# One set of 512-column value products per token mixer, and another order of the projections around it

## The chip, the core and the metric

The kernel runs on one core of a Trainium2 chip. It has five engines that each work through an instruction stream of their own in order: TensorE (PE, matrix products; its weight loads are listed as PEld), VectorE (DVE), ScalarE (ACT), GpSimd (POOL) and SyncE (SP, which here issues nearly all transfers). They wait for one another by semaphores. Products are accumulated in PSUM, a memory of eight banks; everything else lies in SBUF. The metric is the time of one execution on the device, in microseconds (us), and lower is better.

## The reference

Two layers; in each, three token mixers read one normalized input, are merged by sigmoid gates, and are followed by a gated feed-forward block and a gated per-layer input. The change touches the projections `h @ w_in` (in its eight parts), the values `va` and `vc` above all, and the gated product of the convolution.

```python
D_MODEL = 1024; SEQ = 512; DEPTH = 2
HA = 4; DH_A = 64; DV_A = 128; WIDTH_A = 512     # differential attention
CB = 512; CONV_W = 31                            # convolution
HC = 8; DC = 64; WIDTH_C = 512                   # neighbourhood attention
...
    for i in range(DEPTH):
        h = rmsnorm(x, norm_mix[i])
        proj = h @ w_in[i]
        qa, ka, va, glu_in, qc, kc, vc, gates = jnp.split(proj, SPLITS, axis=-1)
        ya = diff_attention(qa, ka, va, lam_q1[i], lam_k1[i], lam_q2[i], lam_k2[i],
                            subln_g[i], lam_init, cos, sin)
        yb = conformer_conv(glu_in, conv_w[i], conv_b[i], cln_g[i], cln_b[i])
        yc = neighbourhood_attention(qc, kc, vc, rpb[i])
        ga, gb, gc = jnp.split(jax.nn.sigmoid(gates), 3, axis=-1)
        merged = (ga * (ya @ w_br_a[i]) + gb * (yb @ w_br_b[i])
                  + gc * (yc @ w_br_c[i]))
        x = x + merged @ w_o[i]
        h = rmsnorm(x, norm_ffn[i])
        x = x + (jax.nn.silu(h @ w_ffn_gate[i]) * (h @ w_ffn_up[i])) @ w_ffn_down[i]
        h = rmsnorm(x, norm_ple[i])
        x = x + jax.nn.sigmoid(h @ w_ple_gate[i]) * (p[i] @ w_ple_in[i])
    return rmsnorm(x, norm_final)
```

In `conformer_conv` the input is first gated, `z = a * sigmoid(g)`, and then convolved along the sequence with 31 taps for each channel. `neighbourhood_attention` has eight heads that the kernel treats in four pairs; `diff_attention` has four heads, whose queries and keys are rotated (rope).

## The kernel before, in words

**Precision.** Every operand of a product is held as a high part and a remainder (suffixes h and l, or hi and lo), and a product is three matmuls: high by high, high by remainder, remainder by high. ACT makes the high part of a weight tile (`wh`, from the loaded `wr`), DVE the remainder (`wl`); each of the three tags has three buffers. A projection (`proj`, `gemm`) gives one [128, 512] result: 8 parts of the model width by 3 matmuls of 512 columns, so 24 matmuls. These are the lines L178, L179 and L180.

**PSUM.** The eight banks are shared out by tags: "mm" has three, "sc" (scores) two, "tr" (transposes) two, "av" (outputs of the attention units) one. A tag hands its banks out in turn, so a new accumulator waits until the one that had the bank three times ago has been read.

**Values.** `values` makes the values of half a mixer's heads: 256 columns, two accumulators of the "mm" tag that each hold two row tiles, 8 parts of the width by 4 row tiles by 3 matmuls of 256 columns (L574, L576, L578): 96 matmuls. It is called twice per mixer (`natten_v(0)`, `natten_v(1)`, `diff_v(0)`, `diff_v(1)`). In the names of the trace these are `natten_mm` and `diff_mm`, like the query and key projections.

**Queries and keys.** `natten_in(pr)` projects a pair's queries and keys. ACT makes the high part (`kh`) out of PSUM and DVE the remainder (`natten_t`), and SP then copies both into stacks (`qk`, `x`) from which the scores are made. For pair 0 of a layer, DVE first multiplies the projection by the row scale (`glu_r` or `ple_r`), since the normalization is not yet applied to the input there; this is what frees the projection's bank. `diff_in(head)` copies the projection by ACT into a buffer of the tag "rp" (`diff_rp`, two buffers, one each for a query or a key); SP copies 32-row blocks for the rotation, DVE multiplies and adds, and the remainder takes the same buffer again, from which SP copies it into the stacks.

**Order.** The order of PE is the order of the code. Attention units (`natten_unit`, `diff_unit`: scores, softmax, transposes, output products) are generators that `later` puts in a queue with a delay in ticks; a tick passes after every four chunks (twelve matmuls of 512 columns) of projection work, so units are dealt out between the projections. The orders of the other engines come from a scheduler that takes their instructions by priority; the convolution's taps (`conv_z`, L161 on DVE) are dealt out behind other instructions by `background`.

**The mixers' stage.** First `glu` makes the four gated blocks of the convolution (j = 0 to 3; each projects a gate and a value), then come the neighbourhood pairs and values, then the differential heads and values, then the gates c and b (`gate_c(m)` and `gate_b(m)`, one projection each).

## Time and profile before

| what | value |
|---|---|
| median of 3 runs (lowest, highest) | 1801.88 us (1801.6, 1803.25) |
| the profiled execution | 1801.18 us, of which the span is 1799.4 us |
| instructions in the span | 27361 |
| PE busy | 1780.7 us, 10404 matmuls |
| DVE busy | 1380.7 us, 2140 instructions |
| ACT busy | 893.1 us, 1495 instructions |
| transfers | 255.98 MB, 142 GB/s |

In the rows of the profile, a name such as `natten_mm` is the phase and the tag of a tile with its number left out, and `a<-b` reads "a is written from b". The span is what the profiler covers; the execution's own time is 1.8 us longer. Busy time of PE is a sum of intervals that overlap in part: the next matmul begins before the last one ends. A timeline row has the start, the duration, the engine, the line and the names, and in brackets the idle time of the engine ahead of it with what ended it; a row of the waits has the sum, the number of times and the longest.

### The profile page before, as it was taken

What the parts mean: (1) busy time and instruction counts of PE and PEld (TensorE: products, weight loads), DVE (VectorE), ACT (ScalarE), POOL (GpSimd) and SP (SyncE); (2) the same over time, 40 slices, a digit from 0 to 9 for tenths busy, and PEclk for the clock granted to TensorE, in tenths of its full rate; (3) what the DMA queues carried; (4) which work ended last, traced back from release to release, by engine and by line L of the source; (5) the groups of instructions that cost most, each with busy time, mean ns of one, the idle gap of its engine ahead of it and who ended that gap; (6) DMA issues with size and microseconds to landing.
All of it is one profiled execution on the core that took longest, in us unless ns stands there. A gap on an engine that the chain in (4) does not pass through costs nothing. (4 is left out here: it accounts for less than half of the span.)

```text
span 1799.4 us, 27361 instructions
## 1 busy us (share of the span) xinstructions
PE 1780.7 (99%) x10404; PEld 1573.4 (87%) x10404; DVE 1380.7 (77%) x2140; ACT 893.1 (50%) x1495; POOL 64.1 (4%) x102
## 2 busy tenths in 40 slices
PE   9999999999999999999999999999999999999998
PEld 7888888888889899898888888888888998998987
DVE  7878887897877577577777878878887775765776
ACT  5467455325565245255545755553255552543554
POOL 0000000000001000000000000000000100000000
PEclk9999999999999999999999999999999999999999
DMA  5566561325646466253437656523374662764432
GB/s 199 165 189 164 150 161 42 103 91 177 198 111 187 138 155 186 81 145 115 157 123 188 187 153 161 128 62 100 97 225 129 156 186 82 192 175 112 115 109 94
DMA packets 98099, 255.98 MB, mean 142 GB/s; under 512 B 12976, under 2 KB 18480, under 8 KB 97968
## 3 DMA queue, kind: packets, MB, share of 16 engines
q1 hardware_dynamic: 90480, 229.62, 41.8%
q0 software_dynamic: 6336, 23.07, 7.3%
q8 instruction: 82, 1.34, 0.3%
q10 hardware_dynamic: 1152, 1.55, 0.3%
q14 instruction: 49, 0.40, 0.1%
HBM read 215.39 MB, written 7.34 MB: 124 GB/s over the span
## 5 line engine op out<-in xcount | busy, mean ns | idle before, releaser
L144 ACT ACTIVATE ffn_wh<-ffn_wr 128x1024 fp32r<-128x1024 f32 (+1 forms) x114 | 117.3, 1029 | 184.9 <-PE ffn_mm L179 101.8
L161 DVE SCALAR_TENSOR_TENSOR conv_z<-glu_z,pre_par,conv_z 128x512 f32<-128x512 f32 x240 | 179.5, 748 | 2.9
L158 DVE TENSOR_TENSOR ffn_wl<-ffn_wr,ffn_wh 128x1024 fp32r<-128x1024 f32 (+1 forms) x114 | 135.0, 1184 | 47.2 <-ACT ffn_wh L144 46.7
L1040 PE MATMUL ffn_sc<-wo_h,ffn_wh 128*128 128x256 f32 x704 | 130.8, 284 | 4.4 <-ACT ffn_pt L144 4.4
L1040 PEld LDWEIGHTS ffn_sc<-wo_h,ffn_wh 128*128 128x128 f32 x704 | 110.1, 192 | 5.8 <-ACT ffn_pt L144 5.3
L1040 PE MATMUL ffn_sc<-wo_h,ffn_wl 128*128 128x256 f32 x352 | 99.6, 283 | 0.0
L178 PE MATMUL ffn_mm<-ffn_z,ffn_wh 128*128 128x512 f32 x240 | 93.4, 389 | 0.0
L179 PE MATMUL ffn_mm<-ffn_z,ffn_wh 128*128 128x512 f32 x240 | 93.4, 389 | 0.0
L180 PE MATMUL ffn_mm<-ffn_z,ffn_wl 128*128 128x512 f32 x240 | 93.4, 389 | 0.0
L158 DVE TENSOR_TENSOR ffn_t<-ffn_mm,wo_r 128x512 f32<-128x512 f32 x48 | 33.1, 689 | 70.6 <-PE ffn_mm L180 70.6
L158 DVE TENSOR_TENSOR ffn_wl<-ffn_rp,ffn_wh 128x1024 fp32r<-128x1024 f32 x44 | 53.8, 1223 | 30.1 <-ACT ffn_wh L144 30.1
L144 ACT ACTIVATE mergea_wh<-mergea_wr 128x1024 fp32r<-128x1024 f32 (+1 forms) x32 | 27.1, 846 | 96.8 <-PE mergea_mm L179 70.8
L1040 PEld LDWEIGHTS ffn_sc<-wo_h,ffn_wl 128*128 128x128 f32 x352 | 67.5, 192 | 0.0
L1040 PE MATMUL ffn_sc<-wo_qk,ffn_wh 128*128 128x256 f32 x352 | 67.1, 283 | 0.0
L1040 PE MATMUL ffn_sc<-wo_v,ffn_wh 128*128 128x256 f32 x352 | 67.1, 283 | 0.0
L1040 PE MATMUL ffn_av<-wo_h,ffn_wh 128*128 128x256 f32 x352 | 65.3, 283 | 0.0
L144 ACT ACTIVATE ffn_wh<-ffn_rp 128x1024 fp32r<-128x1024 f32 x44 | 46.4, 1055 | 30.6 <-PE ffn_mm L179 17.5
L1040 PEld LDWEIGHTS ffn_sc<-wo_qk,ffn_wh 128*128 128x128 f32 x352 | 54.9, 192 | 0.0
L1040 PEld LDWEIGHTS ffn_av<-wo_h,ffn_wh 128*128 128x128 f32 x352 | 54.9, 192 | 0.0
L1040 PEld LDWEIGHTS ffn_sc<-wo_v,ffn_wh 128*128 128x128 f32 x352 | 54.9, 192 | 0.0
L180 PEld LDWEIGHTS ffn_mm<-ffn_z,ffn_wl 128*128 128x128 f32 x240 | 45.1, 188 | 9.5
L178 PEld LDWEIGHTS ffn_mm<-ffn_z,ffn_wh 128*128 128x128 f32 x240 | 45.1, 188 | 9.2
(666 smaller groups left out, 5786.4 us busy)
## 6 DMA issues: line engine op xcount, KB each, us to landing
ffn_wr<-w_gu SPq DMA_DIRECT2D x66, 512.0 KB, 4.3
ffn_e<-w_gu SPq DMA_DIRECT2D x32, 512.0 KB, 3.6
ffn_e<-w_gu POOLq DMA_DIRECT2D x32, 512.0 KB, 7.8
ffn_wr<-w_fd SPq DMA_DIRECT2D x32, 512.0 KB, 4.5
natten_wr<-w_in SPq DMA_DIRECT2D x16, 512.0 KB, 4.3
natten_b<-bias SPq DMA_DIRECT2D x32, 256.0 KB, 2.9
diff_wr<-w_in SPq DMA_DIRECT2D x16, 512.0 KB, 3.7
gatec_wr<-w_in SPq DMA_DIRECT2D x16, 512.0 KB, 3.8
```

What stands on the lines that cost most here:

```text
L144: i = self.nc.scalar.activation(out, in_, func, **kw)
L158: return self.nc.vector.tensor_tensor(out, a, b, op)
L161: return self.nc.vector.scalar_tensor_tensor(out, a, s, b, op0, op1)
L178: mm(out, wh, ah, start=first, stop=False)
L179: mm(out, wh, al, start=False, stop=False)
L180: mm(out, wl, ah, start=False, stop=last)
L1040: mm(bank[:, u], w[:, u, kp], t, start=begin and n == 0, stop=False, skip_group_check=True)
```

## The change

1. `values` makes the values of all heads of a mixer in one set: 96 matmuls of 512 columns, with four accumulators, one per row tile: three of the "mm" tag and the bank of the "av" tag. The set goes over the width in three passes: parts 0 and 1 for the four row tiles, parts 2 and 3, then parts 4 to 7. The value tiles are split per row tile ([128, 512] at a time), and the weights' layout on the host is changed to match.
2. The last gated block (j = 3) leaves `glu`. `glu_last` projects it between the neighbourhood pairs 1 and 2 and copies gate and value by ACT; its sigmoid and product come in `finish`, after the gates' sigmoids.
3. The order of the projections: the neighbourhood values stand behind pair 0, gates c 0 and 1 in front of the differential heads, heads 0 and 1 ahead of the differential values, gates c 2 and 3 ahead of head 3, the other gates behind it. Delays of units change by a tick or two, and the first gate-b tiles take the tag "rp".

```diff
@@ -415,36 +415,38 @@
         self.i, self.h = i, h
         zs, cs = [], []
         self.todo = self.taps(zs, cs)
-        self.glu(zs)
+        self.glu(zs, range(3))
         if i == 0:
             self.lambdas()
         yc, ya, yb = [], [], []
+        acc, gb = [], []
         sn, sd = {}, {}
         self.natten_in(0, sn, yc)
         self.drain(self.renorm)
         self.h = self.hs
-        self.natten_v(0, sn)
+        self.natten_v(sn)
         self.natten_in(1, sn, yc)
-        self.natten_in(2, sn, yc)
-        self.natten_v(1, sn)
-        self.natten_in(3, sn, yc)
-        acc, gb = [], []
-        self.diff_in(0, sd, ya)
-        self.diff_v(0, sd)
-        self.diff_in(1, sd, ya)
-        self.gate_c(acc, 0)
+        finish = self.glu_last(zs)
+        for pr in range(2, 4):
+            self.natten_in(pr, sn, yc)
+        for m in range(2):
+            self.gate_c(acc, m)
+        for head in range(2):
+            self.diff_in(head, sd, ya)
+        self.diff_v(sd)
         self.diff_in(2, sd, ya)
-        self.diff_v(1, sd)
+        for m in range(2, 4):
+            self.gate_c(acc, m)
         self.diff_in(3, sd, ya)
-        for m in range(1, KD):
+        for m in range(4, KD):
             self.gate_c(acc, m)
-        for m in range(2):
+        for m in range(3):
             self.gate_b(gb, m, AF.Copy, None)
-        for g in acc + gb:
+        for g in acc + gb[0:3]:
             self.act(g, g, AF.Sigmoid, table="sigmoid")
+        finish()
         self.branch_c(acc, yc)
-        for m in range(2, 4):
-            self.gate_b(gb, m, AF.Sigmoid, "sigmoid")
+        self.gate_b(gb, 3, AF.Sigmoid, "sigmoid")
         self.merge_a(ya, acc)
         conv = self.run(self.conv(cs, yb))
         pairs = self.inputs()
...
+    def gated(self, z, a, g):
+
+        nc = self.nc
+        mid = z[:, HALO:HALO + GW, :]
+        zc = self.tt(mid.rearrange("p a b -> p (a b)"), a, g, ALU.mult)
+        nc.vector.memset(z[:, 0:HALO, 0:1], 0.0)
+        nc.vector.memset(z[:, HALO + GW:, GR - 1:GR], 0.0)
+        nc.vector.tensor_copy(z[:, 0:HALO, 1:GR], z[:, GW:GW + HALO, 0:GR - 1])
+        nc.vector.tensor_copy(z[:, HALO + GW:, 0:GR - 1], z[:, HALO:2 * HALO, 1:GR])
+        return zc
+
+    def glu_last(self, zs):
+
+        self.phase = "glu"
+        sg = self.sb("r", [P, 512])
+        z = self.sb("z", [P, GW + 2 * HALO, GR])
+        zs.append(z)
+        mid = z[:, HALO:HALO + GW, :].rearrange("p a b -> p (a b)")
+        for out, off in ((sg, CB), (mid, 0)):
+            self.act(out, self.proj(OFF_GLU + off + 3 * P), AF.Copy)
+
+        def finish():
+            self.act(sg, sg, AF.Sigmoid, table="sigmoid")
+            self.gated(z, mid, sg)
+
+        return finish
 
...
@@ -560,33 +583,32 @@
     def values(self, ap, parts):
         mm = self.nc.tensor.matmul
-        accs = [self.ps("mm", (P, 2, 256)) for _ in range(2)]
-        for o in range(0, KD, 4):
-            wh, wl = self.weights(ap[:, o * 256:(o + 4) * 256], 1024)
-            for k in range(o, o + 4):
-                s = slice((k - o) * 256, (k - o + 1) * 256)
-                for t in range(4):
-                    out = accs[t // 2][:, t % 2, :]
-                    ts = slice(t * P, (t + 1) * P)
-                    mm(out, self.h[k][:, 0, ts], wh[:, s], start=k == 0 and t % 2 == 0,
-                       stop=False, skip_group_check=True)
-                    mm(out, self.h[k][:, 0, ts], wl[:, s], start=False, stop=False,
-                       skip_group_check=True)
-                    mm(out, self.h[k][:, 1, ts], wh[:, s], start=False,
-                       stop=k == KD - 1 and t % 2 == 1, skip_group_check=True)
+        accs = [self.ps("mm") for _ in range(3)] + [self.ps("av")]
+        ws = []
+        def products(t, ks):
+            ts = slice(t * P, (t + 1) * P)
+            for k in ks:
+                wh, wl = ws[k // 2]
+                s = slice(k % 2 * 512, k % 2 * 512 + 512)
+                hi, lo = self.halves(self.h[k])
+                mm(accs[t], hi[:, ts], wh[:, s], start=k == 0, stop=False)
+                mm(accs[t], hi[:, ts], wl[:, s], start=False, stop=False)
+                mm(accs[t], lo[:, ts], wh[:, s], start=False, stop=k == KD - 1)
                 self.chunk()
-                self.chunk()
-        vs = []
-        for acc in accs:
-            v = self.sb("v", [P, 2, 512], F32R)
-            for t in range(2):
-                for hi, lo, a in parts(v[:, t], acc[:, t]):
-                    self.split(hi, lo, a)
-            vs.append(v)
-        return vs
+        for o in range(4):
+            ws.append(self.weights(ap[:, o * 1024:(o + 1) * 1024], 1024))
+        for ks in ((0, 1), (2, 3), (4, 5, 6, 7)):
+            for t in range(4):
+                products(t, ks)
+                if ks[-1] == KD - 1:
+                    v = self.sb("v", [P, 2, 512], F32R)
+                    for hi, lo, a in parts(v, accs[t]):
+                        self.split(hi, lo, a)
+                    accs.append(v)
+        return accs[4:]
...
-            self.later(self.natten_unit(pr, n // 2, n % 2, st4, k2, st, box, ys[pr]), 5, 1)
+            self.later(self.natten_unit(pr, n // 2, n % 2, st4, k2, st, box, ys[pr]),
+                       5 if pr else 7, 1)
...
-    def natten_v(self, g, st):
+    def natten_v(self, st):
         self.phase = "natten"
         def parts(v, a):
-            v = v.rearrange("p (u a b c) -> p u a b c", u=2, b=2, c=64)
-            a = a.rearrange("p (u a c) -> p u a c", u=2, c=64)
-            return [(v[:, u, :, u], v[:, u, :, 1 - u], a[:, u]) for u in range(2)]
-        vs = self.values(self.a["w_vc"][self.i, g], parts)
-        vd = self.sb("x", [P, 2, 512], F32R)
-        for n, edge in enumerate((vs[1][0:64, 0], vs[0][64:P, 1])):
-            for o in range(0, P, 64):
-                self.nc.sync.dma_start(vd[o:o + 64, n].bitcast(F32), edge.bitcast(F32))
-        st["v", g] = vs, vd
+            v = v.rearrange("p g (u a b c) -> p u g a b c", u=2, b=2, c=64)
+            a = a.rearrange("p (g u a c) -> p u g a c", g=2, u=2, c=64)
+            return [(v[:, u, :, :, u], v[:, u, :, :, 1 - u], a[:, u]) for u in range(2)]
+        vs = self.values(self.a["w_vc"][self.i], parts)
+        vds = []
+        for g in range(2):
+            vd = self.sb("x", [P, 2, 512], F32R)
+            for n, edge in enumerate((vs[2][0:64, g], vs[1][64:P, g])):
+                for o in range(0, P, 64):
+                    self.nc.sync.dma_start(vd[o:o + 64, n].bitcast(F32), edge.bitcast(F32))
+            vds.append(vd)
+        st["v"] = vs, vds
...
-            gs += self.parts_of("v", [512], 2)
+            gs += self.parts_of("rp" if m < 4 else "v", [512], 2)
...
-            self.later(self.diff_unit(head, qt, st4, k2, st, box, ys), 6 if head else 7, 2)
-    def diff_v(self, g, st):
+            self.later(self.diff_unit(head, qt, st4, k2, st, box, ys), 6, 2)
+    def diff_v(self, st):
         self.phase = "diff"
-        st["v", g] = self.values(self.a["w_va"][self.i, g], lambda v, a: ((v[:, 0:256], v[:, 256:512], a),))
+        def parts(v, a):
+            return [(v[:, :, 0:256], v[:, :, 256:], a.rearrange("p (g c) -> p g c", g=2))]
+        st["v"] = self.values(self.a["w_va"][self.i], parts)
```

The first place to look at is PE in layer 0 where the neighbourhood values begin. In the rows, `natten_mm_603` (before) and `natten_mm_516` (after) are the key projection of pair 0, `natten_mm_650` and `_651` (before) and `natten_mm_575`, `_576`, `_577` and `natten_av_578` (after) the accumulators of the values. Before:

```order
L180 MATMUL natten_mm_603<-glu_b_297,natten_wl_606 128x512
L574 MATMUL natten_mm_650<-natten_wh_653,glu_h_397 128x256 [waits DVE_49,Activation_49]
L576 MATMUL natten_mm_650<-natten_wl_654,glu_h_397 128x256
L578 MATMUL natten_mm_650<-natten_wh_653,glu_h_397 128x256
...
L574 MATMUL natten_mm_651<-natten_wh_653,glu_h_397 128x256 [waits DVE_49]
L576 MATMUL natten_mm_651<-natten_wl_654,glu_h_397 128x256
```

After:

```order
L180 MATMUL natten_mm_516<-glu_b_297,natten_wl_519 128x512
L596 MATMUL natten_mm_575<-natten_wh_580,glu_h_397 128x512 [waits DVE_49,Activation_49]
...
L596 MATMUL natten_mm_576<-natten_wh_580,glu_h_397 128x512 [waits DVE_49]
...
L596 MATMUL natten_mm_577<-natten_wh_580,glu_h_397 128x512 [waits DVE_49]
...
L596 MATMUL natten_av_578<-natten_wh_580,glu_h_397 128x512 [waits PE_49]
```

Six matmuls stand on each accumulator in the first pass; the third, `natten_mm_577`, takes the bank of the key projection `natten_mm_516` and so has a wait on DVE that the two accumulators of before did not have for theirs.

The second place is DVE in the same stretch, where the key projection is read (the `natten_t` row that reads `natten_mm_603` or `natten_mm_516`). Before:

```order
L161 SCALAR_TENSOR_TENSOR conv_z_381<-glu_z_332,pre_par_67,conv_z_381 128x512 [waits DVE_49]
L403 TENSOR_REDUCE glu_lam_544<-glu_t_542 128x4 [waits DVE_49]
L158 TENSOR_TENSOR pre_x_84<-pre_x_84,glu_r_363 128x512
L161 SCALAR_TENSOR_TENSOR natten_t_592<-natten_mm_557,glu_r_363 128x512
L161 SCALAR_TENSOR_TENSOR natten_t_634<-natten_mm_603,glu_r_363 128x512 [waits PE_49]
```

After:

```order
L161 SCALAR_TENSOR_TENSOR natten_t_505<-natten_mm_466,glu_r_363 128x512
...
L158 TENSOR_TENSOR pre_x_84<-pre_x_84,glu_r_363 128x512
L158 TENSOR_TENSOR natten_wl_593<-natten_wr_591,natten_wh_592 128x1024 [waits DMAHW4_49,PE_49,Activation_49]
L161 SCALAR_TENSOR_TENSOR glu_h_486<-pre_x_82,pre_par_67,glu_h_486 128x512 [waits Activation_49]
L161 SCALAR_TENSOR_TENSOR glu_h_502<-pre_x_83,pre_par_67,glu_h_502 128x512 [waits Activation_49]
L161 SCALAR_TENSOR_TENSOR natten_t_505<-natten_t_505,natten_kh_465 128x512 [waits Activation_49]
...
L161 SCALAR_TENSOR_TENSOR glu_h_552<-pre_x_84,pre_par_67,glu_h_552 128x512 [waits Activation_49]
L161 SCALAR_TENSOR_TENSOR conv_z_381<-glu_z_332,pre_par_67,conv_z_381 128x512 [waits DVE_49]
L161 SCALAR_TENSOR_TENSOR natten_t_555<-natten_mm_516,glu_r_363 128x512
```

Before, the query's and the key's reads follow each other and the key's waits for PE; after, fourteen rows stand between the two (rows left out are marked), and the key's read has no wait on PE of its own.

The third place is SP in the differential heads, where head 0's key goes into its stacks (`diff_qk`, `diff_x`): its remainder is `diff_rp_1745` before and `diff_rp_1792` after. Before:

```order
L621 DMA diff_qk_1604<-diff_rp_1745 64x512 [waits DMAHW2_49,DVE_49]
L621 DMA diff_qk_1604<-diff_rp_1745 64x512 [waits DMAHW3_49]
L621 DMA diff_x_1605<-diff_rp_1745 64x512 [waits DMAHW4_49]
L621 DMA diff_x_1605<-diff_rp_1745 64x512 [waits DMAHW5_49]
L172 DMA diff_wr_2379<-w_va 128x1024 [waits DMAHW6_49]
L781 DMA diff_rp_2062<-diff_rp_2062 32x512 [waits DMAHW7_49,Activation_49]
```

After:

```order
L644 DMA diff_qk_1553<-diff_rp_1792 64x512 [waits DMAHW0_49,DVE_49]
L644 DMA diff_qk_1553<-diff_rp_1792 64x512 [waits DMAHW1_49]
L172 DMA diff_wr_2271<-w_in 128x1024 [waits DMAHW2_49,DVE_49]
L644 DMA diff_x_1554<-diff_rp_1792 64x512 [waits DMAHW3_49]
L644 DMA diff_x_1554<-diff_rp_1792 64x512 [waits DMAHW4_49]
L644 DMA diff_qk_1813<-diff_kh_1815 64x512 [waits DMAHW5_49,PE_49,Activation_49]
L644 DMA diff_qk_1813<-diff_kh_1815 64x512 [waits DMAHW6_49]
L644 DMA diff_qk_1813<-diff_rp_1890 64x512 [waits DMAHW7_49,DVE_49]
```

A weight load with a wait on DVE now stands between the four copies of that remainder. On ACT, the copy of head 1's key out of its bank, `diff_rp_1954<-diff_mm_1906`, waits for these copies in the changed order, as it takes the buffer of `diff_rp_1792`:

```order
L144 ACTIVATE diff_wh_1992<-diff_wr_1991 128x1024 [waits DMAHW0_49,PE_49]
L144 ACTIVATE natten_y_1380<-natten_av_1925 64x256 [waits DVE_49,PE_49]
L144 ACTIVATE diff_kh_1815<-diff_rp_1890 128x512 [waits DMAHW4_49,DMAHW5_49,DMAHW2_49,DMAHW6_49,DMAHW1_49,DMAHW7_49,DVE_49,Activation_49]
L144 ACTIVATE diff_rp_1954<-diff_mm_1906 128x512 [waits DMAHW3_49,DMAHW4_49,DMAHW1_49,DMAHW0_49]
L144 ACTIVATE diff_wh_1998<-diff_wr_1997 128x1024 [waits PE_49]
```

The four transfers that `diff_rp_1954` waits for are the four copies out of `diff_rp_1792` that the rows of SP show, two of them behind the weight load; and the third accumulator of the differential values, `diff_mm_1977`, takes the bank of `diff_mm_1906` and waits for this row of ACT.

More of the change, by code (lines that the diff above doesn't have):

```diff
@@ L466, in proj, with glu @@
         return ps
-    def glu(self, zs):
+    def glu(self, zs, js):
         self.phase = "glu"
-        if not self.first:
+        if 0 in js and not self.first:
             self.first = [self.ps("mm") for _ in range(2)]
             self.pair(self.first, [self.a["w_in"][self.i, (OFF_GLU + o) // P] for o in (CB, 0)], self.h)
-        nc = self.nc
-        for j in range(4):
+        for j in js:
             sg, ta = self.sb("t", [P, 512]), self.sb("t", [P, 512])
@@ L488, in value @@
                 self.tt(ta, pa, self.rb, ALU.mult)
-                mid = z[:, HALO:HALO + GW, :]
-                zc = self.tt(mid.rearrange("p a b -> p (a b)"), ta, sg, ALU.mult)
-                nc.vector.memset(z[:, 0:HALO, 0:1], 0.0)
-                nc.vector.memset(z[:, HALO + GW:, GR - 1:GR], 0.0)
-                nc.vector.tensor_copy(z[:, 0:HALO, 1:GR], z[:, GW:GW + HALO, 0:GR - 1])
-                nc.vector.tensor_copy(z[:, HALO + GW:, 0:GR - 1], z[:, HALO:2 * HALO, 1:GR])
+                zc = self.gated(z, ta, sg)
                 if j:
@@ L695, in natten_unit @@
         yield 2
-        vs, vd = st["v", pr // 2]
+        vs, vds = st["v"]
+        g = pr // 2
         if u == 0:
@@ L703, in natten_unit @@
             for k in range(2):
-                mm(av, vs[half][:, n, cols], pp[:, k, n], start=n == k == 0, stop=False)
-        mm(av[:, ws], vd[:, half, cols], p2, start=False, stop=True)
+                mm(av, vs[2 * half + n][:, g, cols], pp[:, k, n], start=n == k == 0, stop=False)
+        mm(av[:, ws], vds[g][:, half, cols], p2, start=False, stop=True)
         qs = slice(half * 256, half * 256 + 256)
@@ L822, in diff_unit @@
             for u in range(2):
-                v = st["v", head // 2][kp][:, u].rearrange("p (a b) -> p a b", a=2)
+                v = st["v"][2 * kp + u][:, head // 2].rearrange("p (a b) -> p a b", a=2)
                 self.mm3(av[:, half * 256:half * 256 + 256], v[:, 0, cs], v[:, 1, cs],
```

4 lines of the change are left out of this document (2 added, 2 removed).

## The prediction

> **What bounds the kernel now.** I read the page's busy rows and clock row first, then the waits of TensorE (PE below), then the timeline at the places that the change touches.
>
> ```profile
> PE 1780.7 (99%) x10404; PEld 1573.4 (87%) x10404; DVE 1380.7 (77%) x2140; ACT 893.1 (50%) x1495; POOL 64.1 (4%) x102
> ...
> PEclk9999999999999999999999999999999999999999
> ...
> PE ffn_sc L1040 <- ACT ffn_pt L144: 4.4, 4, 1.2
> PE natten_av L704 <- DVE natten_y L158: 2.1, 3, 1.4
> PE ffn_tr L214 <- DVE ffn_ss L158: 1.6, 2, 0.8
> PE natten_tr L683 <- DVE natten_pt L158: 1.3, 2, 0.7
> ```
>
> PE is busy 99% of the span at full clock, so time goes only through its instruction stream: cheaper matmuls, or waits put in or taken out. The waits (sum, times, longest, in us) are a few us in 1799.4, so there is little left to win but much room to lose: the stream is one written order, and an instruction that waits holds all behind it. VectorE (DVE) at 77% is the engine that can make it wait; ScalarE (ACT) has half its time free.
>
> **What the wide products save.** The trace's start times give the price of a matmul; durations do not, as the next one starts long before the last one ends.
>
> ```profile
> 51.06 0.39 PE L178 MATMUL natten_mm<-glu_v,natten_wh 128*128 128x512 f32 x1
> ...
> 62.02 0.28 PE L574 MATMUL natten_mm<-natten_wh,glu_h 128*128 128x256 f32 x1
> ...
> 73.52 0.40 PE L178 MATMUL natten_mm<-glu_h,natten_wh 128*128 128x512 f32 x1
> ```
>
> From 51.06 to 62.02 stand 48 matmuls of 512 columns (a query and a key projection, 8 parts of the model width by 3 products each): 10.96 / 48 = 0.228 us each. From 62.02 to 73.52 stand the 96 of 256 columns of one half-mixer's values: 11.50 / 96 = 0.120 each. A mixer now costs 192 x 0.120 = 23.0 us and later 96 x 0.228 = 21.9: 1.1 less, and 2 mixers in 2 layers give -4.3 us (unrounded). The Trainium skill ("TensorE: Matmul & The Clock Gate", section on the back-to-back issue gap) gives a gap of columns / 2.4 ns plus 2.5, so 109 and 216 ns; by it the saving would be 4 x (192 x 0.109 - 96 x 0.216), an estimate of about 1 us. The starts show more for the short form than that rule, and the measured starts are used.
>
> The splits of the values become half as many and twice as long, on ACT and DVE; weight loads and edge copies keep their bytes and counts. All of this lies beside PE's products: nothing on the path. The moved gated block issues the same 48 matmuls, and exchanges two DVE products (with the row scale glu_r) for two ACT copies; its sigmoid and product come late, with ACT half idle. The moved gate-c projections cost the same where they stand. Everything after the gates is unchanged. What matters is what the moves put next to each other.
>
> **Layer 0, the neighbourhood values.** Four accumulators need a fourth bank beside the three of "mm": the set takes all three, and the third (written from the 13th matmul on) is the bank in which the first pair's key projection was left. Before, the gated block's 48 matmuls lay ahead of that projection; now the projection ends at 51.06 and the values follow at once, so the bank is wanted at 51.06 + 12 x 0.228 = 53.8. It is free when DVE has read the projection, and DVE is behind in this stretch: in before it runs without a gap through these rows.
>
> ```profile
> 47.83 0.75 DVE L161 SCALAR_TENSOR_TENSOR conv_z<-glu_z,pre_par,conv_z 128x512 f32<-128x512 f32 x1
> 48.49 0.68 DVE L158 TENSOR_TENSOR pre_x<-pre_x,glu_r 128x512 f32<-128x512 f32 x1
> 49.09 0.75 DVE L161 SCALAR_TENSOR_TENSOR conv_z<-glu_z,pre_par,conv_z 128x512 f32<-128x512 f32 x1
> ...
> 52.27 1.22 DVE L158 TENSOR_TENSOR natten_wl<-natten_wr,natten_wh 128x1024 fp32r<-128x1024 f32 x1
> 53.41 1.29 DVE L158 TENSOR_TENSOR pre_x<-pre_x,glu_r 128x512 f32<-128x512 f32 x2
> ...
> 59.57 0.41 DVE L158 TENSOR_TENSOR glu_t<-glu_t 128x256 f32<-128x256 f32 x1
> 59.91 0.74 DVE L161 SCALAR_TENSOR_TENSOR conv_z<-glu_z,pre_par,conv_z 128x512 f32<-128x512 f32 x1
> 60.57 0.41 DVE L403 TENSOR_REDUCE glu_lam<-glu_t 128x4 f32<-128x256 f32 x1
> 60.90 0.68 DVE L158 TENSOR_TENSOR pre_x<-pre_x,glu_r 128x512 f32<-128x512 f32 x1
> ...
> 62.82 0.15 DVE L158 TENSOR_TENSOR glu_nlam<-glu_lam 128x2 f32<-128x2 f32 x1
> 63.01 0.21 DVE L410 TENSOR_SCALAR glu_nlam<-glu_nlam 128x1 f32<-128x1 f32 x2
> 63.14 1.21 DVE L158 TENSOR_TENSOR natten_wl<-natten_wr,natten_wh 128x1024 fp32r<-128x1024 f32 x1
> ```
>
> DVE's order is the same in both kernels up to the convolution tap at 47.83. From that tap through the key's evacuation the changed order has 12 three-operand instructions at 0.66 (48.49 - 47.83), 4 two-operand ones at 0.60 (49.09 - 48.49), one weight remainder at 1.14 (53.41 - 52.27), one short product and one reduction at 0.34 and 0.33, and three tiny ones, 0.3 in all (63.14 - 62.82): 7.9 + 2.4 + 1.1 + 0.7 + 0.3 = 12.4, so it ends at 60.3. PE waits 60.3 - 53.8 = **+6.5 us**. Only the copies of that key and the score units depend on it besides, and they come 84 matmuls later.
>
> What a wait does to the clock is seen at 77 us of before:
>
> ```profile
> 74.00:83.00 9.00, 7.47 (x27) 5.68 (x26) 3.89 (x13) 4.22 (x13) 0.00 (x0) 0.81 0.81 212
> ...
> 76.04 0.39 PE L180 MATMUL natten_mm<-glu_h,natten_wl 128*128 128x512 f32 x1
> 77.08 0.39 PE L762 MATMUL natten_sc<-natten_qk 128*128 128x256 f32 x1 [0.65 <-DMA natten_qk<-natten_t]
> 78.35 0.39 PE L762 MATMUL natten_sc<-natten_x,natten_qk 128*128 128x256 f32 x1 [0.88 <-DMA natten_x<-natten_t]
> ...
> 78.88 0.63 PE L178 MATMUL natten_mm<-glu_h,natten_wh 128*128 128x512 f32 x1
> ...
> 82.22 0.39 PE L180 MATMUL natten_mm<-glu_h,natten_wl 128*128 128x512 f32 x1
> ...
> 192.22 1.19 SPq L621 DMA_DIRECT2D diff_qk<-diff_rp  x2
> ...
> natten_qk<-natten_t SPq DMA_DIRECT2D x32, 128.0 KB, 3.7
> ```
>
> The window's granted clock is 0.81: eight matmuls from 78.88 to 82.22 take 3.34 us where 8 x 0.228 = 1.82 is the rule, so +1.5 after two short waits. After 6.5 us of wait I put **+1.5** again. The same skill page (section on the clock gate) says that the clock halves after an idle window of about 3.4 us and comes back after as long of work, which would also give about 1.7 us here, an estimate; the trace shows the slow stretch after less idleness than that.
>
> This stretch of before also goes: the first scores then wait for the copies of the first pair's key. PE is ready at 76.27, four short matmuls take 0.5, and it goes on at 78.88: 2.1 of wait and 1.5 of slow clock. In the changed order the 84 matmuls left after 60.3 last 19 us, to 79.5 and more, and the copies, eight issues at 0.6 from about 61.5 and 3.7 to land, are there by 70: **-3.6**. The other waits of the neighbourhood units (2.1 and 1.3 above) are of VectorE's order inside the units, which is nearly the same; from -3.4 (all gone) to +3.4 (doubled), I take 0.
>
> In layer 1 the same bank is asked for in the same way, but DVE is idle there until the projection ends, so it costs nothing:
>
> ```profile
> 944.21 0.69 DVE L158 TENSOR_TENSOR glu_t<-glu_mm,ple_r 128x512 f32<-128x512 f32 x1 [3.35 <-PE glu_mm L180]
> ```
>
> **Both layers, the differential values.** Heads 0 and 1 now follow each other, and the values follow head 1's key projection at once. Their third bank is that projection's, free when ACT has copied it to a "rp" buffer. There are two of these, and the one due holds head 0's key until its low part has been copied to the stacks. The last two of these copies stand in SP's queue behind a weight load (diff_wr) that waits for a remainder (diff_wl), which waits for a high part (diff_wh), whose buffer PE frees at the end of head 1's key.
>
> ```profile
> 186.26 1.06 ACT L144 ACTIVATE diff_wh<-diff_wr 128x1024 fp32r<-128x1024 f32 x1
> ...
> 187.75 0.60 ACT L144 ACTIVATE diff_rp<-diff_mm 128x512 f32<-128x512 f32 x1
> ...
> L158 DVE TENSOR_TENSOR diff_wl<-diff_wr,diff_wh 128x1024 fp32r<-128x1024 f32 x10 | 12.2, 1223 | 5.5 <-ACT diff_wh L144 5.3
> ...
> 177.84 0.58 SPq L172 DMA_DIRECT2D diff_wr<-w_va  x1
> ...
> diff_x<-diff_rp SPq DMA_DIRECT2D x16, 128.0 KB, 2.4
> ```
>
> From the projection's end: 1.06 + 1.22 = 2.3, the load's issue 0.58, the first copy's 0.6 (1.19 for two, above), the second begins at 3.5 and lands 2.4 later at 5.9, ACT's copy 0.6: 6.5. PE wants the bank after five short matmuls (0.6) and 12 x 0.228: at 3.3. Wait 3.2 in each layer: **+6.4**. Just ahead, PE's output products for the last neighbourhood units wait for DVE sums that stand behind the rotation's copies: from 0 to the longest such wait, 1.4, per layer; I take the mean of the three rows that there are, 2.1 / 3 = 0.7: **+1.4**. Slow clock after these waits: 0 to 1.5 per layer (the 1.4 wait of before was followed by none, the pair at 77 was); I take it in one of two, **+1.5**.
>
> Sum: -4.3 + 6.5 + 1.5 - 3.6 + 6.4 + 1.4 + 1.5 = +9.4 us on the profiled execution's 1801.18: 1810.6. The median of the runs stands 0.7 above that execution, so I say 1811.
>
> **Rivals.**
> (A) The banks come free in time: engines run ahead of my hand-played queues, and neither key is late. For it: no bank wait of this kind shows in before, and ACT is half idle. Against it: the queues are in order, DVE's rows above have no gap. Then the plus terms, 6.5 + 1.5 + 6.4 + 1.4 + 1.5 = 17.3, go, and 1801.2 - 7.9 = 1793.3 is left. It decides for faster when less than 45% of these terms is real (then the 7.9 of minus outweighs them).
> (B) About even: the layer-0 wait is real but is paid back, as DVE catches up and the unit waits (3.4) go; and the diff chain costs only half (4.7). 1801.2 - 4.3 + 8.0 - 3.6 - 3.4 + 4.7 = 1802.6.
> (C) DVE falls further back: each wait brings the full slow clock in both layers, units' waits double, and av waits are at 1.4: 1810.6 + 1.5 + 3.4 + 1.4 = 1817 or more.
> (D) Durations, not starts, are the price: 192 x 0.283 - 96 x 0.389 = 17 us per mixer, 1801 - 68 = 1733. The 96 matmuls above, at 0.28 each in only 11.50 us, exclude nearly all of it.
>
> **How the numbers follow.** Forecast 0.56 (its own range 1805.5 to 1816), A 0.20, B 0.14, C 0.09, D 0.01. Within 0.2% is 3.6 us, about what a measurement can tell here, 1798.3 to 1805.5: B, 0.13 with the edges. Faster: A and D with an edge of B, 0.22; slower 0.65. The range 1793 to 1818 leaves out D, the low half of A (0.08) and the top of C (0.05).
>
> **What would show it.** Rows of the new value lines at one start per 0.228 us; a wait of natten_mm on natten_t near 54 us, about 6.5 long, followed by a granted clock under 1 for some us; no wait of the first natten_sc on copies; a wait of diff_mm on ACT diff_rp near 3 in both layers. The forecast is wrong if DVE reads the first key much before 60 us, or if the low-part copies land within 3 us of head 1's key.

## The result, and the profile after

The changed kernel takes 1840.6 us (median of 4 runs, 1840.07 to 1842.47) against 1801.7 for the kernel before, run beside it: a ratio of 1.0225, 95% interval 1.0212 to 1.0238. It is slower by 39 us; the forecast was 9. The two profiled executions, from which the rows below come, lie 41 us apart (1842.5 and 1801.2).

The first lines of the page of the changed kernel, then the waits of PE over the whole run (what waited, for what; sum, times, longest, in us):

```profile
PE 1788.1 (97%) x10020; PEld 1558.3 (85%) x10020; DVE 1374.5 (75%) x2112; ACT 898.1 (49%) x1477; POOL 64.2 (3%) x102
```

```profile
PE diff_mm L596 <- ACT diff_rp L144: 10.5, 2, 5.3
PE natten_av L731 <- DVE natten_y L158: 8.5, 10, 1.8
PE natten_mm L596 <- DVE natten_t L161: 6.2, 1, 6.2
PE diff_av L179 <- DVE diff_pt L158: 5.8, 4, 2.6
...
PE natten_tr L711 <- DVE natten_a L158: 3.0, 3, 1.8
PE natten_sc L789 <- DVE natten_s L685: 2.6, 1, 2.6
...
PE diff_av L178 <- DVE diff_v L158: 0.9, 2, 0.4
PE natten_tr L709 <- DVE natten_pt L158: 0.6, 1, 0.6
PE natten_tr L711 <- ACT natten_e L144: 0.4, 1, 0.4
```

These rows are all in the mixers' stage and sum to 38.5 us. The same stage of before had 5.0 (natten_av 2.1, natten_tr 1.3, natten_sc 0.9 + 0.7). So 33.5 us of waits are new. With the 4.3 us that the wide products save, 39 leaves about 10 for what follows a wait. Most of it is a slow clock (the mean granted clock is 0.991 against 0.998): in this stage, matmuls of 512 columns that start about 0.43 us apart instead of 0.228 add up to 10.7 us of delay, against 1.4 in the kernel before. The two long waits of layer 0 and the clock behind them, from PE's timeline and from the windows around them (of the last three numbers of a window's row, the first is the granted clock):

```profile
60.40 0.79 PE L596 MATMUL natten_mm<-natten_wh,glu_h 128*128 128x512 f32 x1 [6.17 <-DVE natten_t L161]
60.98 0.63 PE L597 MATMUL natten_mm<-natten_wl,glu_h 128*128 128x512 f32 x1
...
65.25 0.47 PE L598 MATMUL natten_av<-natten_wh,glu_h 128*128 128x512 f32 x1
...
192.17 0.39 PE L180 MATMUL diff_mm<-glu_h,diff_wl 128*128 128x512 f32 x1
...
201.22 0.80 PE L596 MATMUL diff_mm<-diff_wh,glu_h 128*128 128x512 f32 x1 [5.29 <-ACT diff_rp L144]
...
205.51 0.40 PE L597 MATMUL diff_av<-diff_wl,glu_h 128*128 128x512 f32 x1
```

```profile
53.80:66.00 12.20, 6.03 (x16) 4.43 (x16) 10.63 (x18) 3.09 (x6) 0.00 (x0) 0.72 0.62 158
195.50:206.00 10.50, 5.21 (x15) 3.78 (x15) 2.06 (x4) 1.23 (x2) 0.00 (x0) 0.67 0.60 151
```

From 60.40 to 65.25 stand 11 starts in 4.85 us instead of 2.5, from 201.22 to 205.51 ten in 4.29 instead of 2.3: 2.3 and 2.0 us of slow clock. In layer 1 the second wait is followed by 2.3 us (11 starts from 1111.74 on), and three stretches behind waits of the neighbourhood units by 4.0 together:

```profile
996.50:1001.00 4.50, 4.50 (x16) 3.55 (x15) 3.16 (x10) 4.40 (x13) 0.00 (x0) 0.62 0.47 160
1007.50:1011.00 3.50, 3.50 (x11) 2.93 (x12) 3.37 (x7) 0.60 (x1) 0.15 (x1) 0.52 0.77 208
1089.50:1092.50 3.00, 3.00 (x9) 2.57 (x10) 2.56 (x9) 2.38 (x7) 0.00 (x0) 0.50 0.77 182
```

### The profile page after: what moved, and what is told of

Its sections match the earlier page's. It is cut to its first block, busy times and chain, and to the rows that moved or that the text cites. A ratio compares the mean times of both kernels' runs of the same rounds, so it can differ in the third digit from the quotient of the medians.

```text
span 1840.7 us, 26541 instructions
## 1 busy us (share of the span) xinstructions
PE 1788.1 (97%) x10020; PEld 1558.3 (85%) x10020; DVE 1374.5 (75%) x2112; ACT 898.1 (49%) x1477; POOL 64.2 (3%) x102
## 5 line engine op out<-in xcount | busy, mean ns | idle before, releaser
L885 DVE TENSOR_REDUCE diff_s<-diff_sc 128x1 f32<-128x512 f32 x64 | 43.3, 684 | 39.5 <-PE diff_sc L789 39.5
```

The costliest lines, as they stand in the source:

```text
L885: nc.vector.tensor_reduce(out=m[:, u:u + 1], in_=sc, op=ALU.max, axis=AX.X, negate=True)
```

## The experiments

All are changes of order, of queue or of how the values are grouped; none leaves out part of the computation. Times are medians; the kernel before stood at 1800 to 1802.5 beside them.

**The last gated block.** One run puts it back in front, the other only makes its sigmoid and product early.

```diff
-        self.glu(zs, range(3))
+        self.glu(zs, range(4))
...
-        finish = self.glu_last(zs)
...
-        finish()
```

> The changed kernel with its last gated block (j = 3) back in front of the first pair, sigmoid and product at once. Bank theory: the 6.2 us wait of the first natten_mm on natten_t and the 2.3 us of slow clock behind it go, since 48 matmuls stand again between DVE's backlog and the key projection: 1840.6 - 8.5 = 1832. Theory that the late product of the block fills DVE at the end of the mixers' stage: the waits of diff_av on diff_pt (2.9 us in each layer, 3.2 by the starts) go as well, -6.4: 1826. If the place of the block did not matter: 1840.

```diff
-        finish = self.glu_last(zs)
+        self.glu_last(zs)()
...
-        finish()
```

> The changed kernel with the sigmoid and the product of the last gated block right behind its projections, which stay where they are. Theory of the late product: only the waits at the end of the stage go (diff_av on diff_pt, 3.2 us in each layer), -6.4: 1834. Rival, these waits come from there being fewer projections behind head 3 than before: no change, 1840.

Measured: 1829.1 and 1838.6. The first lies between its two theories (1832 and 1826), the second between its own (1834 and 1840). With the block in front, the wait of natten_mm on natten_t is gone, and with either edit no wait of diff_av on diff_pt is left. What filled DVE is seen in its timeline at the end of layer 0's stage in the changed kernel:

```profile
334.42 0.68 DVE L158 TENSOR_TENSOR glu_z<-glu_z,glu_r 128x512 f32<-128x512 f32 x1
...
336.42 0.54 DVE L533 TENSOR_SCALAR conv_z<-glu_z,pre_par 128x512 f32<-128x512 f32 x1
...
337.66 0.68 DVE L158 TENSOR_TENSOR branchc_wl<-branchc_wr,branchc_wh 128x512 fp32r<-128x512 f32 x1
338.26 0.75 DVE L161 SCALAR_TENSOR_TENSOR conv_z<-glu_z,pre_par,conv_z 128x512 f32<-128x512 f32 x1
338.92 0.68 DVE L158 TENSOR_TENSOR diff_pt<-diff_tr,diff_pt 128x512 fp32r<-128x512 f32 x1
```

The product of the block (glu_z) comes at 334.42, its taps (conv_z) start at 336.42, and the last differential unit's diff_pt stands between them. The early product gains 2 us and not 6.4, and the intervals of the two ratios overlap, so that this gain is hardly clear of noise. Other waits grew: natten_tr on natten_a and natten_pt from 3.0 + 0.6 to 4.5 + 2.6 us. With the block in front the units' waits grew as well, by 2.4 us, so that 11.5 us are won where both theories together give 14.6. So the late product causes the waits on diff_pt at the end of the stage, but taking them away alone won little time.

**The bank of the differential values.** One run puts 48 matmuls between head 1's key and the values, one only changes the order of copies on SP.

```diff
-        for m in range(2):
-            self.gate_c(acc, m)
         for head in range(2):
             self.diff_in(head, sd, ya)
+        for m in range(2):
+            self.gate_c(acc, m)
         self.diff_v(sd)
...
-            self.later(self.diff_unit(head, qt, st4, k2, st, box, ys), 6, 2)
+            self.later(self.diff_unit(head, qt, st4, k2, st, box, ys), 6 if head else 10, 2)
```

> The changed kernel with gates c 0 and 1 between head 1's projections and the differential values instead of in front of head 0 (head 0's units delayed by the same 4 ticks). Bank theory: the values then find the key's bank free, since 48 matmuls (10.9 us) lie between against a release that took 8; the waits of diff_mm on diff_rp (5.3 and 5.2 us) go, with about 2 us of slow clock after each: -14.5, 1826. Rival, SP and DVE are behind there in any case: the wait moves to the next instruction that needs them, less than 5 us are won, 1836 or more.

```diff
-            self.stack(nat, low, st4[:, 2 * s:2 * s + 2], k2 if s else None)
+            with self.tc.high_priority(offset=150):
+                self.stack(nat, low, st4[:, 2 * s:2 * s + 2], k2 if s else None)
```

> The changed kernel with a higher priority for the copies of the differential stacks; on SP this puts the last two copies of head 0's key remainder ahead of the weight load that waits for VectorE, and changes little else. Theory of the chain through the load: the copies land about 3 us earlier, the waits of diff_mm on diff_rp go from 5.3 to about 2.2 in each layer, 1840.6 - 6.2 = 1834. Rival, the transfers or ScalarE are late in any case: the wait stays at 5, 1840.

Measured: 1834.2 and 1832.9. In the first the waits on diff_rp are gone and those on natten_y are down from 8.5 to 0.7 us, but natten_sc now waits for natten_s 10.9 us instead of 2.6: of the 14.5 us of the bank theory 6.4 are won, and the larger part has moved, as the rival says. The second leaves PE's order alone and does what the chain says; its waits on diff_rp:

```profile
PE diff_mm L596 <- ACT diff_rp L144: 3.9, 2, 1.9
```

So the weight load in SP's queue was worth 6.6 us of wait (10.5 - 3.9), 3.3 in each layer. The timeline of SP and ACT in the changed kernel shows the chain by the numbers:

```profile
194.72 0.33 SPq L172 DMA_DIRECT2D diff_wr<-w_in  x1
195.11 1.10 SPq L644 DMA_DIRECT2D diff_x<-diff_rp  x2
...
200.57 0.60 ACT L144 ACTIVATE diff_rp<-diff_mm 128x512 f32<-128x512 f32 x1 [3.38 <-DMA diff_x<-diff_rp]
```

The transfers of that stretch (the last column is the median time from issue to landing), first in the changed kernel, then with the copies early:

```profile
diff_x<-diff_rp SPq DMA_DIRECT2D x2, 128.0 KB, 4.8
```

```profile
diff_x<-diff_rp SPq DMA_DIRECT2D x2, 128.0 KB, 2.4
```

Measured from ACT's copy of head 0's key, the two transfers are issued 18.4 us later in the changed kernel and 17.3 with the copies early. So about 1 us of the 3.3 is the later issue, and the larger part is that the transfers take 2.4 us longer to land behind the load.

**Wide or early?** Four runs take the wide form and the early place apart: narrow halves in the changed order; and in the order of before, for the neighbourhood values alone, a wide set, two narrow halves together, and the wide set with the first pair's units two ticks later.

```diff
+        for g in range(2):
+            accs = [self.ps("mm", (P, 2, 256)) for _ in range(2)]
...
```

> The changed kernel's order with the values as before in two sets of 256 columns, one right behind the other (the value tiles keep the new form). Bank theory: the waits belong to the set's need for a third and a fourth bank at once; two narrow banks at a time reach the key's bank only with the second set, 11.5 us later, so the waits at the values go (8.5 in layer 0, 7.4 in each layer at the differential values), against 4 x 1.2 us for the narrow form: 1840.6 - 23.3 + 4.9 = 1822. Rival, it is the order alone: the waits stay and the narrow form adds 4.9, 1845.

```diff
-        self.natten_v(0, sn)
+        self.natten_v(sn)
...
-        self.natten_v(1, sn)
```

> The kernel before, with its order, in which only the neighbourhood values are made in one set of 512 columns (value tiles kept by half of the heads, so that the differential values stay as they were). Theory that the order is at fault and not the wide set: 2 x 1.1 us less for the form and no new wait, 1799. Rival, taking the second half of the values out from between the pairs, or holding four weight tiles at once, is what makes the neighbourhood units wait (13 us more in layer 1 of the changed kernel): 1805 to 1812.

```diff
         self.natten_v(0, sn)
+        self.natten_v(1, sn)
...
-        self.natten_v(1, sn)
```

> The kernel before, in which the second half of the neighbourhood values stands right behind the first half (narrow products, two banks, two weight tiles, as they were). Theory that the place is at fault (the second half covered units; moved ahead of them it covers none): the neighbourhood units wait as in the version with one wide set, 10 to 15 us more per layer, 1820 or more. Rival, the wide set is at fault through its four weight tiles and four banks: no more than a wait between the halves of about 4 us per layer (the second half needs the first half's banks), 1803 to 1810.

```diff
-            self.later(self.natten_unit(pr, n // 2, n % 2, st4, k2, st, box, ys[pr]), 5, 1)
+            self.later(self.natten_unit(pr, n // 2, n % 2, st4, k2, st, box, ys[pr]), 5 if pr else 7, 1)
```

> The kernel before with one wide set of neighbourhood values (as in the earlier run) and the first pair's units two ticks later, as the changed kernel has them. Theory that the units only start too early for the values: the waits of natten_sc on the key's copies (4.9 us) and of natten_av on natten_v (3.8 in each layer) go with their slow clock, and little is left, 1805. Theory of the missing cover: these waits go, but the others of the units stay or grow, since the units end later still: 1814 to 1822.

Measured: 1842.4, 1825.5, 1815.3, 1814.2. Narrow halves in the changed order do not help: the second half waits until the first half's banks are read. The waits of the narrow version, then of the two halves in the order of before:

```profile
PE diff_mm L598 <- DVE diff_v L158: 8.4, 2, 4.2
PE natten_mm L598 <- DVE natten_v L158: 6.0, 2, 3.3
```

```profile
PE natten_mm L574 <- DVE natten_v L158: 5.4, 2, 2.7
PE natten_av L704 <- DVE natten_y L158: 5.2, 7, 1.3
```

So the theory that the set's need of four banks makes the waits fell: values that follow at once on what used a bank last wait, wide or narrow. In the order of before, values in one place ahead of the neighbourhood units cost 14 to 15 us, but not for one reason. Of the 15 us of the narrow halves, 5.4 are the waits between the halves, and the units' own waits rose only from 5.0 to 10.5; their time lies between the two expectations. The late wide set has no wait at the banks, and its units wait 16.8 us. In the wide set whose units start 5 ticks later, as in the kernel before, PE waited 7.7 us for natten_v, since the values were not split yet, and 4.5 for the key's copies; with the changed kernel's 7 ticks 2.2 and none are left (1825.5 against 1814.2, 11 us).

**What makes the units wait.** Gates in front of the differential heads, the three edits together, and the bias on another queue:

```diff
-        for m in range(2):
+        for m in range(4):
             self.gate_c(acc, m)
...
-        for m in range(2, 4):
+        for m in range(4, 6):
             self.gate_c(acc, m)
```

> The changed kernel with gates c 0 to 3 in front of the differential heads instead of 0 and 1, gates 4 and 5 behind head 2's projections instead of 2 and 3. Theory that the last neighbourhood units wait because their sums stand on VectorE behind products that wait for the rotation's copies: with 48 matmuls more ahead of head 0, these units are through before the rotation, and the waits of natten_av on natten_y (3.4 us in each layer, some 4.5 by the starts) go: 1840.6 - 9 = 1831. Rival, these units wait for VectorE wherever they stand: 1838 or more.

The next one has this edit, the block in front and the early copies.

> The changed kernel with three edits together: the last gated block back in front, the early stack copies, and gates c 0 to 3 in front of the differential heads. If the waits are separate, what the single edits bring adds up: -11.5 (block, measured) - 6 (copies) - 9 (gates), 1814. If they are one shortage that only moves (too little work of TensorE between the neighbourhood units), less than half of that is won: 1826 or more.

```diff
-            nc.sync.dma_start(b, self.a["bias"][i, head, half])
+            nc.gpsimd.dma_start(b, self.a["bias"][i, head, half])
```

> The changed kernel with the loads of the neighbourhood bias on GpSimd's queue, so that they no longer stand behind weight loads that wait on SP; TensorE's order is the same. Theory of SP's queue: the wait of natten_sc on natten_s in layer 1 (2.6 us) goes with about 2 us of slow clock, and SP is freer at the differential heads; 1834 to 1836. Rival, the units wait for VectorE and ScalarE whatever the bias does: 1840.

Measured: 1854.2, 1848.6, 1844.5, all slower than their theories said, and slower than the changed kernel. The four gates did take the units' waits away (natten_av on natten_y from 8.5 to 2.3 us), but the waits at the bank doubled:

```profile
PE diff_mm L596 <- ACT diff_rp L144: 21.4, 2, 10.9
...
PE natten_av L731 <- DVE natten_y L158: 2.3, 7, 0.5
```

The reason is that PE then got from head 0's key to the values sooner. ACT's copy of that key is the first row below for the changed kernel; the next two are that copy and head 1's in the run with four gates:

```profile
176.73 0.60 ACT L144 ACTIVATE diff_rp<-diff_mm 128x512 f32<-128x512 f32 x1
```

```profile
189.00 0.60 ACT L144 ACTIVATE diff_rp<-diff_mm 128x512 f32<-128x512 f32 x1
...
211.81 0.60 ACT L144 ACTIVATE diff_rp<-diff_mm 128x512 f32<-128x512 f32 x1 [1.99 <-DMA diff_x<-diff_rp]
```

From head 0's copy, PE wanted the bank after 19.2 us in the changed kernel and after 12.9 with four gates, but ACT came to head 1's copy after 23.8 and 22.8. New waits came too: diff_tr on diff_pt 7.0 us, branchc_mm on gatec_x 3.2. Neither in this run nor in the one with all three edits does a weight load stand between the last copies of head 0's key, and in the latter ACT still came only after 22.7 us:

```profile
PE diff_mm L594 <- ACT diff_rp L144: 20.8, 2, 10.5
```

So early copies help where the load stands between them and not here; what holds the chain in this order was not tested.

The bias on its own queue took the wait of natten_sc away, but one of natten_tr on natten_pt (3.7) came in its place, and natten_av waited 11.9 us. The bias did not come clearly earlier in this run: measured from the start of layer 1's value set, its first load behind the set was issued 1.4 us earlier than in the changed kernel and the next about 1 us later. So the run shows that another queue is no cure, and not what a bias in time would be worth.

**The weight tiles that the set holds.** In the changed kernel's layer 1, SP's weight loads (natten_wr) waited until buffers came free at the set's end, with the bias behind them, and DVE's units after that:

```profile
986.73 1.47 SPq L172 DMA_DIRECT2D natten_wr<-w_in  x2
988.29 1.41 SPq L676 DMA_DIRECT2D natten_b<-bias  x2
...
995.35 0.42 DVE L685 CUSTOM_DVE_ANT_0 natten_b<-natten_sc,natten_b 128x256 f32<-128x256 f32 x1 [3.83 <-DMA natten_b<-bias]
...
995.83 0.39 PE L789 MATMUL natten_sc<-natten_qk 128*128 128x256 f32 x1 [2.60 <-DVE natten_s L685]
```

Two runs free one tile earlier, in the changed order and in that of before:

```diff
-        for ks in ((0, 1), (2, 3), (4, 5, 6, 7)):
+        for ks in ((0, 1), (2, 3), (4, 5), (6, 7)):
```

> The changed kernel with the values in four even passes (parts 0 and 1, 2 and 3, 4 and 5, 6 and 7, each over the four row tiles) instead of a last pass over four parts, so that the third weight tile's buffers come free 24 matmuls (5.5 us) earlier. Theory that the wide set makes the neighbourhood units wait by holding two weight tiles to its end: the waits of layer 1 (natten_sc on natten_s 2.6 us, natten_tr on natten_a 2.4) go or shrink to half, with their slow clock, 1834 or less. Rival, they come from the place of the set and the engines' fixed orders, not from the buffers: 1839 or more.

> The kernel before with one wide set of neighbourhood values, the first pair's units two ticks later, and the four even passes. Theory of the held weight tiles: the waits of natten_sc (4.9 us) and natten_tr (4.1) shrink to half, 1808. Rival, place and fixed orders: 1813 or more, as with the uneven passes.

Measured: 1831.2 and 1808.5, so 9.4 and 5.7 us won, the second less surely (1806 to 1809 against 1810 to 1819). In the first, no wait of natten_sc is left, and SP issues the two loads and the bias apart and earlier:

```profile
979.45 0.33 SPq L172 DMA_DIRECT2D natten_wr<-w_in  x1
982.88 0.33 SPq L676 DMA_DIRECT2D natten_b<-bias  x1
984.07 1.11 SPq L665 DMA_DIRECT2D natten_x<-natten_v  x2
985.55 0.33 SPq L172 DMA_DIRECT2D natten_wr<-w_in  x1
986.23 0.33 SPq L676 DMA_DIRECT2D natten_b<-bias  x1
```

The units' waits fell from 15.1 to 10.7 us (natten_av even rose, to 9.3), and the slow clock behind them in layer 1, 4.0 us, was gone. The second run stands 8 us over the kernel before, with 10.4 us of waits in its units against 5.0: that much is left for the place of the set and for what it still holds, its four banks and the last two weight tiles; no run separates the two.

**Do the causes add up?** The block in front with the early copies; these two with the even passes; and, in the order of before, the wide set with late units, even passes and two gates in front of head 0.

> The changed kernel with the last gated block back in front and the early stack copies together. If the two causes are separate: 1840.6 - 11.5 - 7.7 = 1821. If the second only shows because of the first: 1829.

> The changed kernel with three edits whose single gains are measured: the last gated block back in front (-11.5), the early stack copies (-7.7), the four even passes (-9.4). If the three causes are separate, 1840.6 - 28.6 = 1812. If they share their waits, 1818 or more.

```diff
+        for m in range(2):
+            self.gate_c(acc, m)
         self.diff_in(0, sd, ya)
...
-        self.gate_c(acc, 0)
+        self.gate_c(acc, 2)
...
-        for m in range(1, KD):
+        for m in range(3, KD):
```

> The version with one wide set of neighbourhood values in even passes and later first units (1808.5), with gates c 0 and 1 in front of head 0 and gate 2 behind head 1, so that the last neighbourhood units have 10.9 us more of projections before the differential heads. Theory of the missing cover: the waits of these units among the head's projections (about 4 us per layer by the starts, with slow clock some 8 in all) go: 1800 to 1802, level with the kernel before. Rival, the units wait for VectorE wherever they stand, or the differential units miss the two gates behind head 3: 1806 or more.

Measured: 1820.9, 1812.9, 1817.1. The first two add up to a microsecond: block 11.5, copies 7.7 and held tiles 9.4 are separate, and together they explain 28 of the 39 us. The version with all three stands 10 us over the kernel before (ratio 1.0054, 1.0040 to 1.0067). Its largest wait, with 2.1 us in the kernel before, is this:

```profile
PE natten_av L729 <- DVE natten_y L158: 9.8, 7, 2.4
```

All these waits but a short one stand among the projections of heads 0 and 1. The last run does not settle them. It is the version of the order of before with even passes (1808.5), and two gates in front make it 8.6 us slower: its units wait longer, and the end of the stage now lacks the gates (branchc_mm on gateb_v, 4.7). Without the gates and with them:

```profile
PE natten_av L733 <- DVE natten_y L158: 4.4, 5, 1.3
```

```profile
PE natten_av L735 <- DVE natten_y L158: 7.1, 6, 1.5
```

In the changed order four gates took the waits away, in the order of before two did not; whether it is cover or the place of natten_y in DVE's queue stays open. No version beat the kernel before.

## Why the prediction was wrong

The sign was right, and the mechanism in both places that it named. The steps that failed are the term put at nothing for the neighbourhood units, the size of the term for the differential values, and the late product of the moved block, which has no term. Term by term:

- **The wide products**, -4.3: the new lines start every 0.23 us at full clock, as taken. Not the fault.
- **The neighbourhood values in layer 0**, +6.5 and +1.5: 6.2 and 2.3; in layer 1 nothing, as forecast. DVE's queue, added up by hand from the rows of before, ended the key's read at 60.3 (the rows of before do have one gap, 0.17 us at 57.64), and in the changed kernel it did:

```profile
59.66 0.68 DVE L161 SCALAR_TENSOR_TENSOR natten_t<-natten_mm,glu_r 128x512 f32<-128x512 f32 x1
```

- **The first scores' waits**, -3.6: they went; no natten_sc waits in layer 0. By the wait rows and the slow starts they were 1.6 + 1.4 = 3.0.
- **"The other waits of the neighbourhood units ... I take 0"**: this step failed most. The term rested on the order inside the units, which is the same; what changed is what stands around them. natten_av, natten_tr and natten_sc wait 15.1 us now (8.5 + 3.0 + 2.6 + 0.6 + 0.4), 3.4 before without the first scores, so +11.7 where 1.4 was given for all, and 4.0 of slow clock on top. The last units among the heads' projections, which have the 1.4, make 6.8 of the 15.1. The even passes won 9.4 us, of which 4.4 are such waits and 4.0 their slow clock: that much comes from the wide set holding its weight tiles. The rest of these waits, mostly natten_av on natten_y, stays without a shown cause. I had looked for the banks that the set takes and not for the weight buffers that it keeps: three per tag, and two of them read up to the last matmul.
- **The differential values**, +6.4: 10.5, and 0.9 for the values' own split (diff_av on diff_v), and 4.3 us of slow clock (2.0 and 2.3) where 1.5 stood. The chain was right to its last link: the last key matmul starts at 192.17, the second of the copies was to be issued 3.5 us later and stands in the row from 195.11 on. But the copies landed 4.8 us after their issue, and 2.4 was taken, from a median over the kernel; behind the 512 KB load the median did not hold.
- **The moved block's "sigmoid and product come late, with ACT half idle"**: taken at no cost and followed by 5.8 us of waits. ACT was not the limit (its part of diff_pt was done at 334.4); DVE, which makes the product and then 31 taps from it, came to its own part at 338.92.
- Rival C, that DVE falls further back, was the nearest, at "1817 or more" and 0.09; it named the growing waits of the units and the slow clock in both layers. But it was sized by doubling what the rows of before showed, and a wait that a new place makes has no row there.

Added up as measured: -4.3 + 6.2 + 2.3 - 3.0 + 11.7 + 4.0 + 10.5 + 0.9 + 4.3 + 5.8 = +38.4 us, against 38.9 between the medians and 41.3 between the profiled executions.

## What to carry to other kernels

When products are gathered into one larger set, count everything the set holds until its end: accumulators, weight buffers, and what stands in each in-order queue behind a load that waits for them. Work that is finished later brings its followers with it (here the taps on DVE), and these belong in the sum at the place where they land. A wait of 0 for units whose surroundings change is a guess and needs a range of its own. A transfer's landing time is to be taken from rows with the same neighbours in the queue: here the difference, 4.8 against 2.4 us, made a wait of 3.2 us into one of 5.3.

## What the runs showed of the hardware

The 128 KB copies of the key's remainder land in 2.4 us in the median of the kernel before and, in the changed kernel, in 4.8 just behind a 512 KB load from the same queue; issued ahead of it, as the run with the early copies shows, in 2.4. The Trainium skill ("DMA: Bandwidth & Descriptors", section on issuing engines not being separate DMA queues) says that transfers from all issuers run on the same 16 engines and interleave. The slower landing behind the load fits that; both came from SP here, and no run shows it for two issuers.

After a wait of 6.17 us the matmuls started every 0.43 us for 4.85 us, after 5.29 for 4.3, and then at 0.228 again. The Trainium skill ("TensorE: Matmul & The Clock Gate", section on the clock gate) gives half clock after an idle window of about 3.4 us until about as long of work is done; about half the rate agrees, and the return took some 1 to 1.5 us longer here. The slow clock also came behind shorter waits than that window, of 2.60 and 1.84 us in layer 1, for 1.6 and 1.3 us of delay.
